# Eighteen gate and up tiles as pairs of seven products, and a down projection in six passes

## The chip, the core and the metric

The kernel runs on one core of a Trainium2 chip. The metric is the device time of one execution in microseconds; three runs of the kernel before gave 896.15, 896.58 and 896.68, a median of 896.58.

## What is computed

One layer of a decoder, for 520 token columns: 512 of a prompt and one each of 8 sample sequences. Three mixers (pooling, a gated recurrence, chunked gating) share an input projection and are merged; an output projection and a residual follow; then comes the channel mixer, and a last norm. The change is in the channel mixer, which computes, for x after the second norm (width 1024, inner width 3072):

```
g = conv3(x @ wg)              # depthwise over time, width 3, with bias
h = gelu_tanh(g) * (x @ wu)
out = residual + h @ wd        # then the final RMS norm, to the output y
```

All of it is fp32. The second norm divides each token by its root mean square; a gain per feature is folded into x. The state of the convolution is an output too.

## The kernel before

Features lie on the 128 partitions and tokens along the free axis. The 520 tokens are two halves of TH = 260 columns. An fp32 product is made of three products of rounded parts (type F32R): weight high by activation high, weight high by activation low, weight low by activation high. `mm` (lines 115 to 123) issues these for one k of 128 input features: three weight operands by two halves, six matmuls of 128x260 (line 122). A tile of 128 output features with 8 k takes 48 matmuls.

Weights come as chunks of up to 128x1024 fp32 (8 k of one output tile). `Chunk.load` (line 100) issues the DMA from SP into a `raw` buffer; `Chunk.high` (line 106) lets ACT copy it into `wh`; `Chunk.low` (line 112) lets DVE subtract, `wl = raw - wh`. `run_jobs` issues the jobs, one output tile each, in the order in which `job` was called; before a job's matmuls it issues the load, the high and the low of the chunks that lie LOADS = 3, HLEAD = 3 and LLEAD = 2 places ahead. So the queues of SP, ACT and DVE are filled in the order in which the program is written. Each engine runs its queue in order, and an instruction that waits holds all behind it. Work that isn't urgent is put off by `after(n, fn)` until the job counter has gone n further.

A job's sums lie in one PSUM tile of shape [128, 2, 512]: two banks, one per half of the tokens (`PS`, line 70). There are four such tiles. Activations lie in 61 buffers of 128x536.

The channel mixer: `fg_post` (651 to 658) takes the sums of a gate tile off (DVE, times the norm factor). `fg_rest` (660 to 671) makes the convolution: ACT scales and adds the bias (663), DVE adds the two shifted terms (665, two instructions) and the sample columns (667); ACT makes the gelu (669) and DVE multiplies by the norm factor (670). `u2_post` (687) multiplies the up tile's sums by it and splits the result into `h_h` (ACT, 261) and `h_l` (DVE, 262). `dn_post` (692) adds the sums of a down tile to the residual x1, which stays in SBUF. The jobs (726 to 739) go: gate tiles m and m + 1, up tiles m and m + 1, for m up to 11; then a pass of the down projection over these 12 k, 8 output tiles j; then the other 12 m and the second pass. Tiles 6 and 7 of that pass are made for the first half of the tokens, then for the second, so that the final norm of the first half (`sums(0)` and `last(0)`, lines 712 to 724) runs between.

```
        n = 8 if p == 0 else 6
        for js, halves in ((range(n), (0, 1)), (range(n, 8), (0,)), (range(n, 8), (1,))):
            for j in js:
                mid = (TAIL, lambda: n2.append(sums(0))) if halves == (1,) and j == 6 else None
                mid = (0, lambda: last(0, n2.pop())) if halves == (1,) and j == 7 else mid
```

Of the kernel before, what the change touches and what calls it, by code (L numbers as in the profile page):

```python
# [22 lines left out]
KD = D // P  # L23
DP = 512
# [3 lines left out]
HALF = MF // 2  # L28
KW = 6
# [17 lines left out]
# columns of the packed states: h0 (j b), conv (j r b), ffn (m r b), pool (g b r)  # L47
# [5 lines left out]
def trunk_kernel(ctx: ExitStack, tc: tile.TileContext, t: dict, o: dict):  # L53
    nc = tc.nc
    v, s, g, te = nc.vector, nc.scalar, nc.gpsimd, nc.tensor

# [3 lines left out]
    pp = ctx.enter_context(tc.tile_pool(name="pp", bufs=4, space=PSUM))  # L60
    ctx.enter_context(tc.manual_schedule())
# [16 lines left out]
    # ------------------------------------------------------------------ loads  # L78
# [69 lines left out]
    jobs, order = [], []  # L148

    def job(parts, post, pre=None, halves=(0, 1), mid=None):  # L150
        """An output tile: parts [(chunk, tile of the chunk, moving operands by k)], and
        post(psum) that takes the sums off; mid = (k, fn) runs fn before that k"""
        jobs.append((parts, post, pre, halves, mid))
        for c, _, _ in parts:
            if c not in order:
                order.append(c)

    def run_jobs():
        ahead = [(LOADS, "raw", Chunk.load), (HLEAD, "h", Chunk.high), (LLEAD, "l", Chunk.low)]
        at = [0] * 3  # L160
        for n0 in [0, *range(2, len(jobs))]:
            group = jobs[n0:n0 + (2 if n0 == 0 else 1)]
# [3 lines left out]
            i = max(order.index(c) for parts, *_ in group for c, _, _ in parts)  # L166
            for n, (lead, what, fn) in enumerate(ahead):
                while at[n] <= min(i + lead, len(order) - 1):
                    if not hasattr(order[at[n]], what):
                        fn(order[at[n]])  # L170
                    at[n] += 1
            pss = [PS("pj") for _ in group]
            ops = [[(c, a, X, k) for c, a, X in parts for k in range(c.nk)] for parts, *_ in group]
            for n, each in enumerate(zip(*ops)):
                for (c, a, X, k), ps, (_, _, _, halves, mid) in zip(each, pss, group):
                    if mid and mid[0] == n:
                        mid[1]()
                    mm(ps, c.w(k, a), X(k), n == 0, n == len(ops[0]) - 1, halves)
            for ps, each, (_, post, _, halves, _) in zip(pss, ops, group):
                now[0] += len(each) / 8 * len(halves) / 2  # L180
# [10 lines left out]
    # ------------------------------------------------------------------ constants  # L191
# [20 lines left out]
    # state parts of the sample tokens' convolutions  # L212
# [12 lines left out]
    def constants():  # L225
# [8 lines left out]
        # old rows of the sample states  # L234
# [4 lines left out]
    # 4 softplus(-lambda) = 4 (max(-lambda, 0) + log1p(exp(-|lambda|)))  # L239
# [18 lines left out]
    # ------------------------------------------------------------------ helpers  # L258
# [56 lines left out]
    def rstd_psum(r, name):  # L315
        """[m, n] to all partitions, along the tokens"""
# [12 lines left out]
    # ------------------------------------------------------------------ norm 1  # L329
# [15 lines left out]
    # ------------------------------------------------------------------ branch B: conv, RG-LRU  # L345
# [114 lines left out]
    # ------------------------------------------------------------------ branch A: pooling  # L460
# [56 lines left out]
    # ------------------------------------------------------------------ gates and merges  # L517
# [31 lines left out]
    # ------------------------------------------------------------------ branch C: chunked gating  # L549
# [59 lines left out]
    # ------------------------------------------------------------------ branch B: gate, merge  # L609
# [19 lines left out]
    for j in range(8):  # L629
        job([(Chunk(t["w_pb"][j], KD), 0, lambda k: yb[k])], lambda ps, j=j: pb_post(j, ps))  # L630
# [14 lines left out]
    # ------------------------------------------------------------------ channel mixer  # L645
# [5 lines left out]
    def fg_post(m, ps):  # L651
# [5 lines left out]
        v.tensor_mul(two(ext[:, 2:]), acc(ps), two(rs2[0]))  # L657
        fg_rest(m, ext)

    def fg_rest(m, ext):  # L660
# [9 lines left out]
        v.tensor_mul(y, y, rs2[0])  # L670
        fy[m] = y

    def g_post(m, ps):
# [17 lines left out]

    def dn_post(p, j, ps, halves):
        if len(halves) == 2:
            v.tensor_add(two(x1[j]), acc(ps), two(x1[j]))  # L694
            if p == 1:
                if j == 0:
                    nc.scalar.dma_start(o["small"], small)
                    s.activation(root, ones, AF.Sqrt)
                st3[0] = square_add(st3[0], x1[j], f"x2q{j}")
# [26 lines left out]
    for p in range(2):  # L726
        for i in range(HALF // 2):
            for m in (p * HALF + 2 * i, p * HALF + 2 * i + 1):
                job([(Chunk(t["wg"][m], KD), 0, lambda k: xg2[k])], lambda ps, m=m: g_post(m, ps))
            for m in (p * HALF + 2 * i, p * HALF + 2 * i + 1):  # L730
                job([(Chunk(t["wu"][m], KD), 0, lambda k: xg2[k])], lambda ps, m=m: u2_post(m, ps))
        cs = [[(Chunk(t["wd"][p, j, q], KW), 0, lambda k, o=p * HALF + q * KW: hh[o + k]) for q in range(2)]
              for j in range(8)]
        n = 8 if p == 0 else 6
        for js, halves in ((range(n), (0, 1)), (range(n, 8), (0,)), (range(n, 8), (1,))):
            for j in js:
                mid = (TAIL, lambda: n2.append(sums(0))) if halves == (1,) and j == 6 else None
                mid = (0, lambda: last(0, n2.pop())) if halves == (1,) and j == 7 else mid
                job(cs[j], lambda ps, p=p, j=j, halves=halves: dn_post(p, j, ps, halves), None, halves, mid)
# [30 lines left out]
NA, RAW, HS, LS, LOADS, HLEAD, LLEAD = 61, 4, 5, 4, 3, 3, 2  # L770
# [96 lines left out]
```

## Time and profile before

| What | us |
| --- | --- |
| median of three runs | 896.58 |
| the profiled execution's span, first to last instruction | 895.0 |
| PE busy | 884.0 (99%) |
| DVE busy | 525.2 (59%) |
| ACT busy | 344.0 (38%) |
| POOL busy | 56.1 (6%) |

The profile shows one execution, whose span is 895.0 us; its time with what lies around the span isn't given apart, so the median of the runs, 1.6 us more, stands for it. The shares are averages over the whole span. DMA moved 86.12 MB, and the mean granted TensorE clock was 0.996 of full speed. POOL sends three small DMAs of its own; SP sends all the weights.

### The profile page before, as it was taken

What the parts mean: (1) busy time and instruction counts of PE and PEld (TensorE: products, weight loads), DVE (VectorE), ACT (ScalarE), POOL (GpSimd) and SP (SyncE); (2) the same over time, 40 slices, a digit from 0 to 9 for tenths busy, and PEclk for the clock granted to TensorE, in tenths of its full rate; (3) what the DMA queues carried; (4) which work ended last, traced back from release to release, by engine and by line L of the source; (5) the groups of instructions that cost most, each with busy time, mean ns of one, the idle gap of its engine ahead of it and who ended that gap; (6) DMA issues with size and microseconds to landing.
All of it is one profiled execution on the core that took longest, in us unless ns stands there. A gap on an engine that the chain in (4) does not pass through costs nothing.

```text
span 895.0 us, 16824 instructions
## 1 busy us (share of the span) xinstructions
PE 884.0 (99%) x7358; PEld 880.8 (98%) x7358; DVE 525.2 (59%) x779; ACT 344.0 (38%) x456; POOL 56.1 (6%) x93
## 2 busy tenths in 40 slices
PE   9999999999999999999999999999999999999995
PEld 8999999999999999999999999999999999999995
DVE  5897998689665442155555666653234555554345
ACT  7554573776342342222334433332122333333210
POOL 1403311111100000000000000000000000000000
PEclk9999999999999999999999999999999999999998
DMA  9423233133232223222321422222332223323212
GB/s 293 152 99 107 73 106 98 57 96 95 72 118 72 94 92 122 71 72 95 95 94 48 131 89 90 88 71 90 106 113 77 95 94 94 95 71 116 74 37 96
DMA packets 28298, 86.12 MB, mean 96 GB/s; under 512 B 3112, under 2 KB 6312, under 8 KB 28200
## 3 DMA queue, kind: packets, MB, share of 16 engines
q1 hardware_dynamic: 26752, 83.21, 29.1%
q10 hardware_dynamic: 1376, 1.44, 0.5%
q8 instruction: 58, 0.95, 0.4%
q0 software_dynamic: 96, 0.39, 0.1%
q14 instruction: 16, 0.13, 0.0%
HBM read 82.63 MB, written 2.79 MB: 95 GB/s over the span
## 4 chain that ended last, share of the span: by engine, by line
PE 98%; DVE 1%; DMA 0%; ACT 0%; issue 0%; DVEq 0%
PE pj L122 95%; PE lru L122 1%; DVE y L722 1%; PE vm L581 0%; DMA par<-in_par 0%; PE po L122 0%; PE vt L574 0%; PE n30p L293 0%; DVE x2q L705 0%; DVE x L703 0%; PE n1p L293 0%; PE nvp L293 0%; PE n2p L293 0%; ACT xg_h L756 0%; PE n31p L293 0%; DVE n L309 0%
## 5 line engine op out<-in xcount | busy, mean ns | idle before, releaser
L112 DVE TENSOR_TENSOR wl<-raw,wh 128x1024 fp32r<-128x1024 f32 (+2 forms) x162 | 182.4, 1136 | 32.5 <-ACT wh L106 32.2
L106 ACT ACTIVATE wh<-raw 128x1024 fp32r<-128x1024 f32 (+2 forms) x162 | 156.7, 975 | 58.5 <-PE pj L122 55.5
L122 PE MATMUL pj<-x_h,wh 128*128 128x260 f32 x768 | 154.6, 283 | 0.0
L122 PE MATMUL pj<-x_h,wl 128*128 128x260 f32 x768 | 154.3, 282 | 0.0
L122 PE MATMUL pj<-x_l,wh 128*128 128x260 f32 x768 | 154.3, 282 | 0.0
L122 PE MATMUL pj<-xn_h,wh 128*128 128x260 f32 x704 | 142.1, 283 | 0.0
L122 PE MATMUL pj<-xn_l,wh 128*128 128x260 f32 x704 | 141.8, 283 | 0.0
L122 PE MATMUL pj<-xn_h,wl 128*128 128x260 f32 x704 | 141.5, 282 | 0.0
L122 PEld LDWEIGHTS pj<-x_h,wl 128*128 128x128 f32 x768 | 118.5, 188 | 0.0
L122 PEld LDWEIGHTS pj<-x_l,wh 128*128 128x128 f32 x768 | 118.1, 188 | 0.0
L122 PEld LDWEIGHTS pj<-x_h,wh 128*128 128x128 f32 x768 | 117.9, 188 | 0.0
L122 PEld LDWEIGHTS pj<-xn_h,wl 128*128 128x128 f32 x704 | 108.5, 188 | 0.0
L122 PEld LDWEIGHTS pj<-xn_h,wh 128*128 128x128 f32 x704 | 108.4, 189 | 0.0
L122 PEld LDWEIGHTS pj<-xn_l,wh 128*128 128x128 f32 x704 | 108.3, 188 | 0.0
L122 PE MATMUL pj<-h_h,wl 128*128 128x260 f32 x384 | 81.3, 283 | 0.0
L122 PE MATMUL pj<-h_h,wh 128*128 128x260 f32 x384 | 81.3, 283 | 0.0
L122 PE MATMUL pj<-h_l,wh 128*128 128x260 f32 x384 | 81.1, 282 | 0.0
L122 PEld LDWEIGHTS pj<-h_h,wl 128*128 128x128 f32 x384 | 60.9, 188 | 0.0
L122 PEld LDWEIGHTS pj<-h_l,wh 128*128 128x128 f32 x384 | 60.8, 188 | 0.0
L122 PEld LDWEIGHTS pj<-h_h,wh 128*128 128x128 f32 x384 | 60.8, 188 | 0.0
L694 DVE TENSOR_TENSOR x<-pj,x 128x520 f32<-128x520 f32 x14 | 9.8, 699 | 77.2 <-PE pj L122 77.2
L665 DVE SCALAR_TENSOR_TENSOR fc<-fg,par,fc 128x512 f32<-128x512 f32 x48 | 36.1, 752 | 18.9 <-ACT fc L663 18.0
(277 smaller groups left out, 1208.7 us busy)
## 6 DMA issues: line engine op xcount, KB each, us to landing
raw<-in_w_in SPq DMA_DIRECT2D x50, 512.0 KB, 3.6
raw<-in_wg SPq DMA_DIRECT2D x24, 512.0 KB, 3.5
raw<-in_wu SPq DMA_DIRECT2D x24, 512.0 KB, 3.5
raw<-in_wd SPq DMA_DIRECT2D x32, 384.0 KB, 3.1
raw<-in_w_pb SPq DMA_DIRECT2D x8, 512.0 KB, 3.5
raw<-in_w_o SPq DMA_DIRECT2D x8, 512.0 KB, 3.6
x<-in_x SPq DMA_DIRECT2D x8, 260.0 KB, 4.6
raw<-in_w_pa SPq DMA_DIRECT2D x4, 512.0 KB, 3.4
```

What stands on the lines that cost most here:

```text
L106: s.activation(self.h[:, q], self.raw[:, q], AF.Copy)
L112: v.tensor_sub(self.l[:, q], self.raw[:, q], f(self.h[:, q]))
L122: te.matmul(ps[:, h, :TH], ww, xx[:, h * TH:(h + 1) * TH], start=first and n == 0, stop=last and n == 2)
L665: v.scalar_tensor_tensor(y[:, :SEQ], ext[:, r:r + SEQ], pc("fcw", r * MF + m), y[:, :SEQ], op0=ALU.mult, op1=ALU.add)
L694: v.tensor_add(two(x1[j]), acc(ps), two(x1[j]))
L722: v.scalar_tensor_tensor(y[:, j - j0, :], x1[j][:, c], pc("gf", j), ps[:, 0, :TH], op0=ALU.mult, op1=ALU.mult)
```

## The change

Gate tiles 6 to 23 become nine pairs, and so do up tiles 6 to 23. The two tiles of a pair are a 2 by 2 block product: two output tiles by two halves of the tokens, and the 8 k as two halves of 4 k. Seven products of such blocks are made in place of eight (Winograd's form of Strassen's algorithm). The moving operands are sums and differences of normalised activations X0 to X8, made once in `operands()`; the weights are h1 (as loaded), h2 and h3 (sums that DVE makes) and h0 (a half, as loaded). A product is 12 matmuls of 128x260: 4 k by three part products.

- In `run_pair` the products P0, P2, P4 and P6 lie in bank 0 of a PSUM tile `pa`, P1 in bank 1 of the same tile, P3 and P5 in a tile `pc`. ACT copies four partial sums off (line 252): A1 after P0, A2 after P2, C1 after P3, A3 after P4. DVE makes c21 (bank 1 minus A1) after P1, then c12 (from SBUF) and c22; c11 is taken off after P6.
- The low part of h1 and h0, and of the weights of gate and up tiles 0 to 5, is made without DVE: a negated copy of the high part (POOL for h1 and h0, ACT for tiles 0 to 5), and then an accumulating DMA from POOL that adds the weights from DRAM.
- The down projection runs in six passes of 4 k. Pass p - 1 lies between the pairs of pass p: two down tiles behind each gate pair and two behind each up pair. For passes 0 to 4 ACT copies the sums off (line 946) and an accumulating DMA from POOL adds them to the residual, which now lies in DRAM. SP loads that back ahead of the last pass.
- In the last pass tiles 0 to 3 are made whole, then tiles 4 to 7 for the first half of the tokens, then for the second.
- Gate tiles 4 to 23 read normalised activations, so that the two multiplications by the norm factor fall away for them.
- There are 55 activation buffers in place of 61, and 5 of `wl` in place of 4.

```diff
+        PRODUCTS = ((("h1", 0), 0, 0), (("h1", 1), 1, 1), (("h3", 0), 2, 0), (("h2", 0), 3, 2),
+                    (("h2", 1), 4, 0), (("h3", 1), 5, 2), (("h0", 0), 6, 0))
...
+    def low_by_dma(eng, l, h, src):
+        if eng is s:
+            s.activation(l, f(h), AF.Copy, scale=-1.0)
+        else:
+            eng.tensor_scalar(l, f(h), -1.0, None, op0=ALU.mult)
+        nc.gpsimd.dma_start(l, src, accum_op=ALU.add)
...
+        def high1(self):
+            h, l = self.new("h1")
+            s.activation(h, self.raw[1], AF.Copy)
+            low_by_dma(NEG, l, h, self.src[1])
...
+        def steps(self):
+            return ((-3.5, self.load), (-2.2, self.high1), (-1.75, self.sums), (-1.3, lambda: self.high("h3")),
+                    (-1.05, lambda: self.high("h2")), (-0.8, self.high0), (-0.8, lambda: self.low("h3")),
+                    (-0.55, lambda: self.low("h2")))
...
+    def run_pair(n):
+        pair, X, out = pairs[n]
+        af, c = PS("pa"), PS("pc")
+        bank = (af[:, 0, :TH], af[:, 1, :TH], c[:, 0, :TH])
+        m, k = A("m"), A("k")
+        kept = {"A1": m[:, :TH], "A2": m[:, TH:], "A3": k[:, :TH], "C1": k[:, TH:]}
+        seen, t0 = [0, 0, 0], now[0]
+        for i, (b, ops) in enumerate(pair.products(X)):
+            for j, (w, x) in enumerate(ops):
+                for e, (ww, xx) in enumerate(((w[0], x[0]), (w[0], x[1]), (w[1], x[0]))):
+                    te.matmul(bank[b], ww, xx, start=seen[b] + j + e == 0, stop=i >= (6, 1, 5)[b] and j == 3 and e == 2,
+                              skip_group_check=True)
+            seen[b] += 1
+            now[0] = t0 + 0.25 * (i + 1)
+            if (b, seen[b]) in ((0, 1), (0, 2), (0, 3), (2, 1)):
+                s.activation(kept["AFC"[b] + str(seen[b])], bank[b], AF.Copy)
+            for a, fn in {1: ("c21", lambda: (bank[1], kept["A1"])), 4: ("c12", lambda: (kept["A3"], kept["C1"])),
+                          5: ("c22", lambda: (bank[2], kept["A2"])), 6: ("c11", lambda: (bank[0], None))}.items():
+                if a == i:
+                    out(fn[0], *fn[1]())
...
+            if n == "c11":
+                s.activation(o_, a, AF.Copy)
+                fg_rest(m, ext[0])
+                return
+            v.tensor_sub(o_, a, b)
+            if n == "c22":
+                after(0.2, lambda: fg_rest(m + 1, ext[1]))
...
     def dn_post(p, j, ps, halves):
+        if p < NP - 1:
+            y = A(f"dn{j}")
+            s.activation(two(y), acc(ps), AF.Copy)
+            nc.gpsimd.dma_start(x1d[:, j, :], y, accum_op=ALU.add)
+            return
...
+            if halves == (1,):
+                mid = {4: (3, lambda: n2.append(sums(0))), 6: (3, lambda: last(0, n2.pop()))}.get(j)
...
+    for p in range(NP):
+        for i in range(2):
+            m = p * KW + 2 * i
+            wg_jobs(m, m >= MN)
+            wd_jobs(p - 1, (4 * i, 4 * i + 1))
+            wu_jobs(m, m >= MN)
+            wd_jobs(p - 1, (4 * i + 2, 4 * i + 3))
+    wd_jobs(NP - 1, range(4))
+    for h in range(2):
+        for j in range(4, 8):
+            wd_job(NP - 1, j, (h,))
```

The order of the instructions on the engines, at three places. First PE at the start of a gate tile before (tile 10); `pj` is the tile's PSUM, `x1..h` and `x1..l` the parts of the moving operand, and "waits" names the engines or queues whose semaphores an instruction waits for.

```order
L122 MATMUL pj_6742<-x17_l_5439,wh_6552 128x260 x2
L122 MATMUL pj_6742<-x17_h_5438,wl_6620 128x260 x2
L122 MATMUL pj_6808<-x10_h_4998,wh_6618 128x260 [waits PE_49,Activation_49]
L122 MATMUL pj_6808<-x10_h_4998,wh_6618 128x260
L122 MATMUL pj_6808<-x10_l_4999,wh_6618 128x260 x2
L122 MATMUL pj_6808<-x10_h_4998,wl_6680 128x260 [waits DVE_49]
L122 MATMUL pj_6808<-x10_h_4998,wl_6680 128x260
L122 MATMUL pj_6808<-x11_h_5060,wh_6618 128x260 x2
```

And PE in the changed kernel at the gate pair of tiles 6 and 7, where its products P0, P1, P2 and P3 begin (X00 and X01 belong to P0, X1 to P1, X2 to P2, X3 to P3).

```order
L247 MATMUL pa_6525<-X00_h_6270,wh_6372 128x260 [waits DVE_49,Activation_49,Pool_49]
L247 MATMUL pa_6525<-X00_l_6271,wh_6372 128x260 [waits Pool_49]
...
L247 MATMUL pa_6525<-X01_h_6306,wl_6373 128x260
L247 MATMUL pa_6525<-X1_0h_5958,wh_6372 128x260 [waits Activation_49]
...
L247 MATMUL pa_6525<-X1_1h_5960,wl_6373 128x260
L247 MATMUL pa_6525<-X2_0h_6111,wh_6431 128x260 [waits DVE_49]
L247 MATMUL pa_6525<-X2_0l_6112,wh_6431 128x260
...
L247 MATMUL pa_6525<-X2_1h_6113,wl_6432 128x260
L247 MATMUL pc_6526<-X3_0h_6048,wh_6453 128x260 [waits PE_49]
L247 MATMUL pc_6526<-X3_0l_6049,wh_6453 128x260
```

Before, a tile waited at its start and at its first low part. Now the first matmul of P1 waits for ACT (its copy A1 of bank 0), and that of P2 for DVE (its c21 from bank 1), in each of the 18 pairs; P3's wait on PE is for the earlier user of `pc`.

Second, ACT's queue before, around gate tiles 8 and 9 (`fc` is the convolution and the gelu, `h` the product's high part).

```order
L663 ACTIVATE fc8_6543<-fg8_6539,par_77 128x512 [waits DVE_49,Pool_49]
L669 ACTIVATE fc8_6543<-fc8_6543 128x520 [waits DVE_49]
L106 ACTIVATE wh_6552<-raw_6550 128x1024 [waits DMAHW7_49,PE_49,Activation_49]
L663 ACTIVATE fc9_6609<-fg9_6605,par_77 128x512 [waits DVE_49,Pool_49]
L669 ACTIVATE fc9_6609<-fc9_6609 128x520 [waits DVE_49]
L106 ACTIVATE wh_6618<-raw_6616 128x1024 [waits DMAHW0_49,PE_49,Activation_49]
L261 ACTIVATE h8_h_6672<-fc8_6543 128x520 [waits DVE_49]
L106 ACTIVATE wh_6678<-raw_6676 128x1024 [waits DMAHW1_49,PE_49,Activation_49]
L261 ACTIVATE h9_h_6732<-fc9_6609 128x520 [waits DVE_49]
L106 ACTIVATE wh_6738<-raw_6736 128x1024 [waits DMAHW2_49,PE_49,Activation_49]
```

And in the changed kernel, from the gate pair of tiles 8 and 9 to the up pair behind it (`dn` are the down tiles' sums; `m` from `pa_7131` are A1 and A2 of the up pair).

```order
L907 ACTIVATE fg8_7011<-pa_6927 128x260 [waits PE_49,Activation_49]
L804 ACTIVATE fc8_7046<-fg8_7011,par_79 128x512 [waits DVE_49,Activation_49,Pool_49]
L810 ACTIVATE fc8_7046<-fc8_7046 128x520 [waits DVE_49]
L179 ACTIVATE wh_7052<-sum_6992 128x1024
L804 ACTIVATE fc9_7056<-fg9_6958,par_79 128x512
L810 ACTIVATE fc9_7056<-fc9_7056 128x520 [waits DVE_49]
L165 ACTIVATE whq_7075<-raw_6877 128x512 [waits DMAHW2_49]
L946 ACTIVATE dn0_7097<-pj_7062 128x520 [waits PE_49]
L116 ACTIVATE wh_7114<-raw_7030 128x1024 [waits DMAHW4_49]
L946 ACTIVATE dn1_7128<-pj_7101 128x520 [waits PE_49]
L252 ACTIVATE m_7133<-pa_7131 128x260 [waits PE_49]
L252 ACTIVATE m_7133<-pa_7131 128x260 [waits DVE_49,PE_49]
```

Before, the gelu of a tile stood between copies of weights. Now the two convolutions, the two gelus, three copies of weights and two of down sums stand between c11 of the gate pair and A1 of the up pair.

Third, DVE's queue in the tail before, behind the first half's sums (`n30` is the norm of the first half).

```order
L311 TENSOR_TENSOR n30l_9838<-n302_9836,n30h_9837 65x4 [waits DVE_49]
L300 TENSOR_TENSOR n30d1_9840<-ident_84,n30l_9838 65x260 [waits DVE_49]
L703 TENSOR_TENSOR x6_75<-pj_9812,x6_75 128x260 [waits PE_49]
L705 TENSOR_TENSOR x2q61_9875<-x6_75 128x260 [waits DVE_49]
L707 TENSOR_TENSOR x2q0_9276<-x2q0_9276,x2q61_9875 128x260 [waits DVE_49]
L722 SCALAR_TENSOR_TENSOR y00_9882<-x0_69,par_77,n30b_9879 128x260 [waits PE_49]
L722 SCALAR_TENSOR_TENSOR y01_9885<-x1_70,par_77,n30b_9879 128x260
```

And in the changed kernel at the same place.

```order
L441 TENSOR_TENSOR n30l_10354<-n302_10352,n30h_10353 65x4 [waits DVE_49]
L430 TENSOR_TENSOR n30d1_10356<-ident_86,n30l_10354 65x260 [waits DVE_49]
L958 TENSOR_TENSOR xe4_10133<-pj_10331,xe4_10133 128x260 [waits PE_49]
L960 TENSOR_TENSOR x2q41_10370<-xe4_10133 128x260 [waits DVE_49]
L962 TENSOR_TENSOR x2q0_10169<-x2q0_10169,x2q41_10370 128x260 [waits DVE_49]
L958 TENSOR_TENSOR xe5_10135<-pj_10373,xe5_10135 128x260 [waits PE_49]
L960 TENSOR_TENSOR x2q51_10387<-xe5_10135 128x260 [waits DVE_49]
L962 TENSOR_TENSOR x2q0_10169<-x2q0_10169,x2q51_10387 128x260 [waits DVE_49]
L977 SCALAR_TENSOR_TENSOR y00_10403<-xe0_10125,par_79,n30b_10400 128x260 [waits PE_49]
L977 SCALAR_TENSOR_TENSOR y01_10406<-xe1_10127,par_79,n30b_10400 128x260
```

Before, one tile's residual stood between the norm and the first half's y; now it is two tiles', and two more follow behind the eight y.

## Rows read from the trace of the kernel before

**Rows 1.** The profile page: busy us (share) and instructions; then the chain by engine

```profile
PE 884.0 (99%) x7358; PEld 880.8 (98%) x7358; DVE 525.2 (59%) x779; ACT 344.0 (38%) x456; POOL 56.1 (6%) x93
...
PE 98%; DVE 1%; DMA 0%; ACT 0%; issue 0%; DVEq 0%
```

**Rows 2.** The chain that ended last, in order of time: start us, us, engine, what

```profile
36.87 34.63 PE pj L122 x288
...
480.17 395.37 PE pj L122 x3300
875.54 0.89 PE n30p L293 x16
...
884.91 0.65 PE n31p L293 x8
```

**Rows 3.** Timeline of PE at its last dense matmuls: start us, us, engine, line, instruction, out<-in

```profile
883.53 0.28 PE L122 MATMUL pj<-h_l,wh 128*128 128x260 f32 x1
883.65 0.28 PE L122 MATMUL pj<-h_h,wl 128*128 128x260 f32 x1
```

**Rows 4.** Groups of instructions by line and shape: busy us, mean ns, then idle before them

```profile
L112 DVE TENSOR_TENSOR wl<-raw,wh 128x1024 fp32r<-128x1024 f32 x122 | 150.0, 1232 | 31.9 <-ACT wh L106 31.6 <-issue 0.3
...
L106 ACT ACTIVATE wh<-raw 128x1024 fp32r<-128x1024 f32 x122 | 127.6, 1049 | 22.7 <-PE pj L122 21.0 <-DMA raw<-in_w_in 1.7
...
L663 ACT ACTIVATE fc<-fg,par 128x512 f32<-128x512 f32 x24 | 19.6, 817 | 70.5 <-DVE fg L657 66.0 <-DVE fg L681 2.3 <-DVE small L661 2.1
...
L261 ACT ACTIVATE h_h<-fc 128x520 fp32r<-128x520 f32 x24 | 15.3, 639 | 65.9 <-DVE fc L689 65.9
...
L522 ACT ACTIVATE gt<-pj 128x520 f32<-128x520 f32 x24 | 14.5, 605 | 82.2 <-PE pj L122 78.0 <-issue 4.2
```

**Rows 5.** Timeline of ACT in the channel mixer, 520 to 527 us

```profile
521.23 0.82 ACT L663 ACTIVATE fc<-fg,par 128x512 f32<-128x512 f32 x1 [4.22 <-DVE fg L657]
523.79 0.64 ACT L669 ACTIVATE fc<-fc 128x520 f32<-128x520 f32 x1 [1.74 <-DVE fc L667]
524.33 1.05 ACT L106 ACTIVATE wh<-raw 128x1024 fp32r<-128x1024 f32 x1
```

**Rows 6.** Timeline of DVE in the tail, from 878 us

```profile
878.21 0.42 DVE L300 TENSOR_TENSOR n30d<-ident,n30l 65x260 fp32r<-65x260 f32 x1
879.44 0.43 DVE L703 TENSOR_TENSOR x<-pj,x 128x260 f32<-128x260 f32 x1 [0.80 <-PE pj L122]
...
880.71 3.25 DVE L722 SCALAR_TENSOR_TENSOR y<-x,par,n30b 128x260 f32<-128x260 f32 x8
883.97 0.43 DVE L703 TENSOR_TENSOR x<-pj,x 128x260 f32<-128x260 f32 x1
884.43 0.43 DVE L705 TENSOR_TENSOR x2q<-x 128x260 f32<-128x260 f32 x1
```

**Rows 7.** DMA issues: out<-in, queue, operation, KB each, us from issue to landing

```profile
raw<-in_wg SPq DMA_DIRECT2D x24, 512.0 KB, 3.5
...
out_pool_old<-in_state_pool POOLq DMA_DIRECT2D x1, 224.0 KB, 5.3
```

**Rows 8.** Groups of POOL's instructions by line and shape, as rows 4

```profile
L396 POOL TENSOR_SCALAR q<-q 128x520 f32<-128x520 f32 x8 | 8.8, 1096 | 108.6 <-DVE q L395 108.6
...
L235 POOL DMA_DIRECT2D out_pool_old<-in_state_pool x1 | 0.8, 776 | 0.0
```

**Rows 9.** Busy time in one-us windows near the end: PE, PEld, DVE, ACT, POOL, granted clock

```profile
883.00:884.00 1.00, 1.00 (x13) 1.00 (x12) 1.00 (x4) 0.00 (x0) 0.00 (x0) 1.00 0.93 312
...
887.00:888.00 1.00, 0.51 (x2) 0.31 (x2) 0.75 (x3) 0.00 (x0) 0.00 (x0) 1.00 0.03 7
888.00:889.00 1.00, 0.35 (x1) 0.06 (x1) 0.61 (x2) 0.00 (x0) 0.00 (x0) 0.51 0.00 0
```

**Rows 10.** Timelines of DVE and then of POOL, 95 to 112 us

```profile
105.07 1.90 DVE L112 TENSOR_TENSOR wl<-raw,wh 128x1024 fp32r<-128x1024 f32 x1
...
104.82 4.43 POOL L482 TENSOR_TENSOR ps<-ps 128x524 f32<-128x524 f32 x3
```

More of the change, by code (lines that the diff above doesn't have):

```diff
@@ L23 @@
 KD = D // P
+KW = 4
 DP = 512
@@ L27 @@
 MF = FF // P
-HALF = MF // 2
-KW = 6
 EPS = 1e-6
@@ L148, in trunk_kernel, with at, pair_job @@
     jobs, order = [], []
+    pairs = {}
+    def at(t, fn):
+        later.append((t, len(later) + done[0], fn))
+    def pair_job(pair, X, out):
+        pairs[len(jobs)] = (pair, X, out)
+        jobs.append(None)
+    def run_pair(n):
[18 more added lines that the diff above has]
+                    out(fn[0], *fn[1]())
+            run_later(now[0] + 1e-6)
     def job(parts, post, pre=None, halves=(0, 1), mid=None):
@@ L154, in job @@
         for c, _, _ in parts:
-            if c not in order:
+            if c not in order and not c.timed:
                 order.append(c)
@@ L159, in run_jobs @@
         ahead = [(LOADS, "raw", Chunk.load), (HLEAD, "h", Chunk.high), (LLEAD, "l", Chunk.low)]
-        at = [0] * 3
+        begun = [0] * 3
+        t1 = 0
+        for n, e in enumerate(jobs):
+            if e is None:
+                for dt, fn in pairs[n][0].steps():
+                    at(t1 + dt, fn)
+                t1 += 1.75
+                continue
+            parts, _, _, halves, _ = e
+            for c, _, _ in parts:
+                if c.timed and not hasattr(c, "raw") and not hasattr(c, "due"):
+                    c.due = t1
+                    for lead, fn in zip((4, 3, 2.9) if c.by_dma else (3, 2, 1.5), (c.load, c.high, c.low)):
+                        at(t1 - lead, fn)
+            t1 += sum(c.nk for c, _, _ in parts) / 8 * len(halves) / 2
         for n0 in [0, *range(2, len(jobs))]:
+            if n0 in pairs:
+                run_pair(n0)
+                continue
             group = jobs[n0:n0 + (2 if n0 == 0 else 1)]
@@ L165, in run_jobs @@
                     pre()
-            i = max(order.index(c) for parts, *_ in group for c, _, _ in parts)
+            timed = group[0][0][0][0].timed
+            i = max([order.index(c) for parts, *_ in group for c, _, _ in parts if not timed], default=-9)
             for n, (lead, what, fn) in enumerate(ahead):
[L168 to L171, printed above, removed]
+                while begun[n] <= min(i + lead, len(order) - 1):
+                    if not hasattr(order[begun[n]], what):
+                        fn(order[begun[n]])
+                    begun[n] += 1
             pss = [PS("pj") for _ in group]
@@ L178, in run_jobs @@
                     mm(ps, c.w(k, a), X(k), n == 0, n == len(ops[0]) - 1, halves)
+                if timed and n < len(ops[0]) - 1:
+                    now[0] += len(halves) / 16
+                    run_later(now[0] + 1e-6)
             for ps, each, (_, post, _, halves, _) in zip(pss, ops, group):
-                now[0] += len(each) / 8 * len(halves) / 2
+                now[0] += (1 if timed else len(each)) / 8 * len(halves) / 2
                 post(ps)
@@ L656, in fg_post @@
             return ext
-        v.tensor_mul(two(ext[:, 2:]), acc(ps), two(rs2[0]))
+        if m < MN:
+            v.tensor_mul(two(ext[:, 2:]), acc(ps), two(rs2[0]))
+        else:
+            s.activation(two(ext[:, 2:]), acc(ps), AF.Copy)
         fg_rest(m, ext)
@@ L682, in g_post @@
                 fg_rest(i, x)
+            after(0.25, operands)
     n2 = [None]
@@ L724, in last @@
             (nc.sync if i % 2 == 0 else nc.scalar).dma_start(o["y"][:, j0:j0 + n, c], y)
[L726 to L735, printed above, removed]
-            for j in js:
-                mid = (TAIL, lambda: n2.append(sums(0))) if halves == (1,) and j == 6 else None
-                mid = (0, lambda: last(0, n2.pop())) if halves == (1,) and j == 7 else mid
-                job(cs[j], lambda ps, p=p, j=j, halves=halves: dn_post(p, j, ps, halves), None, halves, mid)
+    XP = [op_of(n) for n in range(7)]
```

189 lines of the change are left out of this document (174 added, 15 removed).

## The prediction

> **What bounds it now.** I read the page first, for the engine that is full, then the chain of waits, for whether its time is work, then timelines, for the price of one step. PE is busy 884.0 us and is 98% of the chain that ended last [rows 1]. Within the chain 288 matmuls take 34.63 us and 3300 take 395.37 us [rows 2], so a matmul costs 0.120 us, with no pause for another engine. Two things follow: each matmul left out saves 0.120 us, and each wait put into PE's queue is paid in full, since nothing else is behind it. A single matmul takes 0.28 us from start to end while the next starts after 0.12 us [rows 3]. So a PE that must wait for the result of its last matmul loses 0.28 - 0.12 = 0.16 us of draining ahead of any handoff.
>
> **What is saved.** A pair before is 96 matmuls (2 tiles of 48) and now 84 (7 products of 12). That is 12 x 18 = 216 fewer, 216 x 0.120 = 25.9 us. The down projection has as many matmuls in six passes as in two.
>
> **What is added, first part: two waits in each pair.** The order of PE's queue shows that P1's first matmul waits for ACT's copy A1, and P2's for DVE's c21, since both banks are one tile. P0 ends just ahead of P1, so this isn't hidden. P1's wait is draining 0.16, handoff to the reader 0.04 (a matmul ends at 883.65 + 0.28 = 883.93 [rows 3] and DVE starts at 883.97 [rows 6]), the copy, and the handoff back, 0.05 (884.86 to 884.91 [rows 2, 6]). The copy of 128x260 from PSUM isn't in the trace. The copy of 128x520 is 0.605; two SBUF copies, 1.049 for 1024 columns and 0.639 for 520, give 0.81 ns per column [rows 4], so 0.605 - 0.21 = 0.39. Its ends are 0.30 (half of 0.605) and 0.605 (no gain). P1 loses 0.16 + 0.04 + 0.39 + 0.05 = 0.64 us. P2's wait has a DVE subtraction of 128x260 in place of the copy, 0.43 [rows 6]: 0.68 us. P3's wait is for an earlier user of the other PSUM tile, long done. P4, P5 and P6 wait for copies issued a whole product (1.44 us) earlier, so there are some 0.4 us to spare. A pair with two such waits takes 84 x 0.12 + 0.64 + 0.68 = 11.40 us.
>
> **Second part: ACT's queue ahead of each up pair.** I count from the start of a gate pair. It ends at 11.40; the two down tiles behind it take 48 x 0.12 = 5.76, so the up pair starts at 17.16, and P1 could start one product later, at 18.60. A1 of that up pair stands on ACT behind everything in the order's rows:
> - c11 starts at 11.60 and ends at 11.99; the first convolution starts at 12.01.
> - A convolution's start to its gelu's start is 523.79 - 521.23 = 2.56 us, as DVE's two shifted terms lie between; the gelu to the next start is 0.54 us [rows 5], which is 0.10 less than its own 0.64.
> - I take off this 0.10 for each ACT instruction that follows another: copies of 1024 columns 0.95, of 512 (1.049 - 512 x 0.81 ns = 0.63) 0.53, of down sums 0.51.
> - So: gelu 14.57, h2's copy 15.11, second convolution 16.06, its gelu 18.62, h0's copy 19.16, down sums 19.69, down weights 20.20, down sums 21.15, A1 from 21.66 to 22.05, P1 at 22.10.
>
> P1 waits 22.10 - 18.60 = 3.50 us instead of 0.64. Behind the up pair stand two high parts in place of convolution and gelu, and no step there waits 2.56 us, so ACT has caught up by the next gate pair. A cycle of a gate and an up pair then loses 0.64 + 0.68 + 3.50 + 0.68 = 5.50 us, and nine cycles 49.5 us.
>
> **Third part: the tail.** Before, 60 matmuls followed the sums for the first half's norm; now 39 do, so 21 x 0.12 = 2.5 us of PE's work stand ahead of that point. From its start to the end the kernel took 895.0 - 875.54 = 19.46 us [rows 2]. Now: the norm's steps on DVE end 3.09 us later (878.63); two tiles' residual steps, 1.27 each (879.44 to 880.71); eight y, 3.26 (to 883.97); tile 6, 1.27; tile 7 up to the second sums, 0.94 (to 884.91); from there to the end 10.09, as before [rows 2, 6]. That makes 3.09 + 2.54 + 3.26 + 1.27 + 0.94 + 10.09 = 21.19 us. The tail costs 21.19 - 19.46 + 2.5 = 4.2 us; if DVE's order didn't matter it would cost nothing.
>
> **What costs nothing.** Copies and additions of the down sums (ACT, POOL's DMAs): nobody waits for the DMA before the last pass, and the copies' place on ACT is counted above. DVE's four sums per pair and low parts: before, DVE was busy 59% [rows 1], and it lost the two multiplications of each gate tile; without that cover it would delay c21, at 1.23 us for each low part [rows 4]. POOL's negations can slow DVE: beside POOL's additions a low part took 1.90 us [rows 10] and not 1.23; they fall mostly where ACT's queue is late anyhow.
>
> **The sum.** 895.0 - 25.9 + 49.5 + 4.2 = 922.8 us of span; the median of the runs lies 1.6 us above the span, so 924.4 us. My own range for this case: 915 (copies of 0.30, ACT gaining another 0.5 us per cycle, no cost in the tail) to 935 (copies of 0.605, no overlap of 0.10 on ACT).
>
> **Rivals.**
> *Accumulating DMAs that land late.* The trace has none. h1's low part is needed by the third matmul of the next pair. In a gate pair h1's copy follows A2 and ends near 7.2 us; POOL's negation of 1024 columns takes two of 1.10 (520 columns), the DMA's issue 0.78 [rows 8], so the issue ends at 10.2, and 7.2 us are left to 17.4; the up pair leaves about as much. A plain load of 512 KB lands in 3.5 us, POOL's own DMA of 224 KB in 5.3 [rows 7], and by size that would be 12.1 for 512 KB. I take about 6, nearer to the first, since POOL's 224 KB came from DRAM to DRAM, so no loss. At 12.1 each gate pair waits 4.9 us and each up pair 4.9 less some 2.9 that its ACT backlog hides: 9 x (4.9 + 2.0) = 62, giving 986 us.
> The Trainium skill, page DMA: Bandwidth & Descriptors, section on the anatomy of one DMA on the SWDGE path, fits 2.0 us plus bytes over 436 GB/s for one DMA. By that 512 KB would be an estimated 3.2 us and this rival would fall; but the 224 KB row has 5.3 where the fit has 2.5, so the trace does not agree.
>
> *The clock falls in the gaps.* In the tail the granted clock was 1.00 up to 888 us and 0.51 in the next microsecond, the lower level, 1.2 GHz, about 4 us after the last dense matmul at 883.93 [rows 3, 9], with only a few small ones between. The gap of 3.50 us is about that long. If it fell and P1 and P2 ran at the lower level, 24 matmuls would cost 0.12 more each, 2.9 us x 9 = 26: 950 us. Against: 3.5 is under 4, and PE is dense on both sides.
> The Trainium skill, TensorE: Matmul & The Clock Gate, section on HAM oscillation, describes a kernel with idle stretches of a few microseconds between bursts, each of which started at the lower clock. By that rule this rival is the forecast; here only the end of the kernel shows such a fall.
>
> *No backlog.* If ACT reached A1 in time, only the bare waits stayed: 18 x 1.32 = 23.8, and 895.0 - 25.9 + 23.8 + 4.2 + 1.6 = 898.7, 2.1 us over the median and at the edge of what can be told from no change. It needs ACT's queue between c11 and A1 to be 2.9 us shorter, with two steps of 2.56 us that DVE sets.
>
> *Faster.* P1 and P2 write where nobody reads just then, and if their waits are met while matmuls still drain, the saving stays. It decides below (25.9 - 4.2) / 18 = 1.21 us lost per pair. With the bare copy and subtraction alone, 0.82 per pair, the time is 895.0 - 25.9 + 14.8 + 4.2 + 1.6 = 889.7; with no loss 874.9. For it speaks ACT's 38% [rows 1]; against it, that the waits stand in the order's rows and draining is a measured 0.16.
>
> That the saving isn't made at all can't be: the queue holds 216 matmuls less.
>
> **How the numbers follow.** Forecast 0.62, clock 0.11, late DMAs 0.12, no backlog 0.05, faster 0.10. The predicted time is the forecast's, 924.4. The range, 897 to 952, takes in the forecast's 915 to 935, no backlog and the clock; left out are the faster case (0.10) and most of the late DMAs (0.10). A measurement of this kernel can tell 0.2%, 1.8 us: faster 0.10, same 0.05, slower 0.85.
>
> **What would show it.** In the profile after: PE's idle ahead of P1 and P2 named as released by ACT and DVE, 0.64 and 0.68 us, and about 3.5 us ahead of each up pair's P1; PE busy about 858 us; ACT without a pause from c11 to the up pair's A1. Wrong would be PE waiting at a pair's third matmul for a DMA queue, a granted clock under 1.00 after the gaps, or idle of PE below 1.2 us per pair.

## The result, and the profile after

The changed kernel takes 961.36 us (median of 4 runs, 958.49 to 965.64) against 896.63 us for the kernel before: a ratio of 1.0725, with a 95% interval from 1.0697 to 1.0754. It is slower, as forecast, but by 64.7 us and not by 28; the time lies outside the range. The profiled execution's span is 963.9 us.

The page of the changed kernel, its busy times, its granted clock in 40 slices and its chain, answers to [rows 1].

```profile
PE 893.8 (93%) x7142; PEld 880.6 (91%) x7142; DVE 576.4 (60%) x894; ACT 438.5 (45%) x633; POOL 235.5 (24%) x237
...
PEclk9999999999999999999999988987999879999797
...
PE 75%; DVE 9%; ACT 9%; issue 4%; DMA 2%; POOL 0%; DVEq 0%; ACTq 0%
```

PE executes fewer matmuls and yet reads busier than 884.0 us; the clock row says why: of its last 17 slices, eight show a 7 or an 8, that is, a mean clock under 0.9. PE's share of the chain fell from 98% to 75%: now other engines release it. The waits of PE, largest first (us in total, times, longest):

```profile
PE pa L247 <- ACT m L252: 35.0, 18, 3.4
PE pa L247 <- DVE c L929: 5.3, 9, 0.6
PE pa L247 <- DVE fg L910: 5.2, 9, 0.6
PE pa L247 <- DMA wl<-in_wg: 5.1, 1, 5.1
...
PE pj L200 <- DVE wl L125: 3.9, 1, 3.9
```

The first three are the forecast's: 18 waits for A1, 9 and 9 for c21. The waits of 5.1 and 3.9 us are single ones, at the third matmul of the first pair and in the first down tiles. Cycles of a gate and an up pair on PE's timeline (start us, us; in brackets the idle ahead and its releaser):

```profile
604.47 0.39 PE L247 MATMUL pa<-X_0h,wh 128*128 128x260 f32 x1 [0.54 <-ACT m L252]
...
606.76 0.39 PE L247 MATMUL pa<-X_0h,wh 128*128 128x260 f32 x1 [0.58 <-DVE fg L910]
...
624.78 0.39 PE L247 MATMUL pa<-X_0h,wh 128*128 128x260 f32 x1 [3.42 <-ACT m L252]
...
627.14 0.59 PE L247 MATMUL pa<-X_0h,wh 128*128 128x260 f32 x1 [0.59 <-DVE c L929]
...
644.89 0.39 PE L247 MATMUL pa<-X_0h,wh 128*128 128x260 f32 x1 [0.47 <-ACT m L252]
...
665.15 0.58 PE L247 MATMUL pa<-X_0h,wh 128*128 128x260 f32 x1 [3.37 <-ACT m L252]
...
686.28 0.39 PE L247 MATMUL pa<-X_0h,wh 128*128 128x260 f32 x1 [0.54 <-ACT m L252]
...
706.59 0.39 PE L247 MATMUL pa<-X_0h,wh 128*128 128x260 f32 x1 [3.43 <-ACT m L252]
...
708.91 0.39 PE L247 MATMUL pa<-X_0h,wh 128*128 128x260 f32 x1 [0.59 <-DVE c L929]
...
723.99 0.39 PE L247 MATMUL pa<-X_0h,wh 128*128 128x260 f32 x1 [0.48 <-ACT m L252]
```

P1 and P2 of the gate pair at 604.47 and 606.76 wait 0.54 and 0.58 us, P1 and P2 of the up pair at 624.78 and 627.14 wait 3.42 and 0.59. The idle is counted from the modelled end of the last matmul; with the draining of 0.16 us of [rows 3] these are 0.70, 0.74, 3.58 and 0.75 us. From one gate pair's P1 to the next it takes 40.42 us (604.47 to 644.89), 41.39 (to 686.28) and 37.71 (to 723.99). The 264 matmuls of a cycle, at 0.12 us each, are worth 31.68 us. The 37.7 are a cycle at full clock, and they hold 6.0 us of waits.

What the longer cycles have beyond that shows in one-us windows of the first (the length of the window; busy time of PE, PEld, DVE, ACT and POOL; then the granted clock):

```profile
620.00:621.00 1.00, 1.00 (x11) 1.00 (x10) 0.96 (x2) 0.00 (x0) 0.00 (x0) 1.00 0.00 0
622.00:623.00 1.00, 0.00 (x0) 0.00 (x0) 1.00 (x2) 1.00 (x4) 0.38 (x1) 1.00 0.00 0
...
626.00:627.00 1.00, 0.54 (x5) 0.27 (x3) 0.35 (x2) 0.00 (x0) 1.00 (x3) 0.64 0.90 156
627.00:628.00 1.00, 0.86 (x4) 0.87 (x5) 0.96 (x3) 0.00 (x0) 0.96 (x2) 0.50 0.92 221
632.00:633.00 1.00, 1.00 (x7) 1.00 (x6) 0.00 (x0) 0.26 (x1) 1.00 (x1) 0.50 1.03 199
...
634.00:635.00 1.00, 1.00 (x11) 1.00 (x10) 0.15 (x1) 0.57 (x2) 0.70 (x2) 1.00 0.37 148
```

PE idled from 621.36 to 624.78. The clock was still granted in full in that time and a microsecond beyond, then fell to 0.50, the lower level of 1.2 GHz, until about 633. There the matmuls of P2 and P3 run at half speed: P2's first takes 0.59 us in the rows at 627.14 and 0.39 at 708.91, where the clock stayed up. Over the nine cycles the clock fell in seven, at 2.7 to 3.7 us each; the cycles from 686 and from 806 us had the same idle of 3.4 us and kept it.

### The profile page after: what moved, and what is told of

Read it like the earlier page. It is cut to its first block, busy times and chain, and to the rows that moved or that the text cites. A ratio compares the mean times of both kernels' runs of the same rounds, so it can differ in the third digit from the quotient of the medians.

```text
span 963.9 us, 16992 instructions
## 1 busy us (share of the span) xinstructions
PE 893.8 (93%) x7142; PEld 880.6 (91%) x7142; DVE 576.4 (60%) x894; ACT 438.5 (45%) x633; POOL 235.5 (24%) x237
## 4 chain that ended last, share of the span: by engine, by line
PE 75%; DVE 9%; ACT 9%; issue 4%; DMA 2%; POOL 0%; DVEq 0%; ACTq 0%
PE pj L200 53%; PE pa L247 13%; PE pc L247 6%; DVE fc L806 3%; ACT fc L804 2%; ACT wh L116 2%; DVE wl L125 1%; PE lru L200 1%; ACT fc L810 1%; ACT dn L946 1%; DMA wl<-in_wg 1%; ACT wh L179 1%; DVE y L977 1%; ACT whq L165 1%; DMA x<-in_x 1%
## 5 line engine op out<-in xcount | busy, mean ns | idle before, releaser
L125 DVE TENSOR_TENSOR wl<-raw,wh 128x1024 fp32r<-128x1024 f32 (+1 forms) x106 | 124.2, 1177 | 38.6 <-ACT wh L116 38.6
L116 ACT ACTIVATE wh<-raw 128x1024 fp32r<-128x1024 f32 (+1 forms) x118 | 117.7, 1004 | 10.5 <-PE pj L200 7.7
L247 PE MATMUL pa<-X_0h,wh 128*128 128x260 f32 x108 | 38.5, 357 | 45.5 <-ACT m L252 35.0
L247 PEld LDWEIGHTS pa<-X_0h,wh 128*128 128x128 f32 x108 | 23.8, 220 | 53.7 <-ACT m L252 38.8
L97 POOL TENSOR_SCALAR wl<-wh 128x1024 fp32r<-128x1024 f32 x18 | 50.3, 2792 | 75.3 <-ACT wh L160 75.3
L97 POOL TENSOR_SCALAR wlq<-whq 128x512 fp32r<-128x512 f32 x18 | 34.6, 1923 | 120.0 <-ACT whq L165 120.0
L252 ACT ACTIVATE m<-pa 128x260 f32<-128x260 f32 x36 | 13.9, 387 | 100.2 <-PE pa L247 100.2
L652 ACT ACTIVATE gt<-pj 128x520 f32<-128x520 f32 x24 | 14.5, 605 | 83.0 <-PE pj L200 83.0
L183 DVE TENSOR_TENSOR wl<-sum,wh 128x1024 fp32r<-128x1024 f32 x36 | 46.3, 1325 | 0.0
```

The costliest lines, as they stand in the source:

```text
L97: eng.tensor_scalar(l, f(h), -1.0, None, op0=ALU.mult)
L116: s.activation(self.h[:, q], self.raw[:, q], AF.Copy)
L183: v.tensor_sub(l, self.s[n], f(h))
L247: te.matmul(bank[b], ww, xx, start=seen[b] + j + e == 0, stop=i >= (6, 1, 5)[b] and j == 3 and e == 2, skip_group_check=True)
L252: s.activation(kept["AFC"[b] + str(seen[b])], bank[b], AF.Copy)
L652: s.activation(two(y), acc(ps), AF.Sigmoid)
```

## The experiments

Theory: what the forecast lacks is the low clock, and the long idle ahead of an up pair's P1 causes it; ACT is late there because it waits for DVE between convolution and gelu. Rivals: the clock falls from the short pauses or the load of DMA and POOL; ACT is short of time; the six passes and accumulating DMAs cost the time.

**A tile of its own for P1's bank.**

```diff
-        af, c = PS("pa"), PS("pc")
-        bank = (af[:, 0, :TH], af[:, 1, :TH], c[:, 0, :TH])
+        af, ag, c = PS("pa"), PS("pb"), PS("pc")
+        bank = (af[:, 0, :TH], ag[:, 0, :TH], c[:, 0, :TH])
```

> The bank of P1 becomes a PSUM tile of its own, so P1 no longer waits for the copy A1; P2 does, because it adds to bank 0. Theory (the late A1 idles PE and the long idle lowers the clock): the two short waits of a gate pair go, the wait of an up pair moves to P2 and shrinks from 3.4 to about 2.0 us, and an idle of 2 us leaves the clock at 1.00: 9 x 3 = 27 us less idle and about 34 us less at the low clock, near 900 us. Rival (the clock falls for another reason, the short waits apart: the load of DMA and POOL, or the single-bank products): the idle goes, the low clock stays, near 934 us.

914.24 us, ratio 1.0193 (1.0173 to 1.0213). PE's waits for ACT in the pairs:

```profile
PE pa L247 <- ACT m L252: 17.6, 9, 2.0
```

Nine in place of 18, none over 2.0 us, and behind only one of these nine (at 755 us) did the clock fall, for 3 us. The time fell by 47.1 us, where the rival had 27. It is 14 us above the 900 expected, mostly since the low clock had been priced at 34 us, too much, as the run after next shows; four waits of up to 0.9 us for the low part of h0 are new.

**The second convolution behind A1.**

```diff
-                after(0.2, lambda: fg_rest(m + 1, ext[1]))
+                after(1.5, lambda: fg_rest(m + 1, ext[1]))
```

> Only the convolution and gelu of the second tile of a gate pair are put behind A1 of the up pair on ACT. Theory: A1 comes on time, the wait of 3.4 us becomes 0.5 as in a gate pair, and the clock stays at 1.00: 9 x 2.9 = 26 us of idle and some 34 us of low clock go, near 901 us. Rival (the clock falls with the pauses of 0.5 us or the load): 26 us go and the clock still falls, near 935 us. Rival two (ACT is simply short of time): the convolution behind A1 now delays A2 and the 3 us come back at P4, near 961 us.

922.64 us, ratio 1.0287 (1.0266 to 1.0307). PE's waits in the pairs:

```profile
PE pa L247 <- DVE c L929: 9.4, 9, 1.1
PE pa L247 <- ACT m L252: 8.8, 18, 0.5
```

A1 is on time, as expected (0.5 at the longest). But c21 of the up pairs now waits up to 1.1 us and not 0.6, as DVE's terms of the moved convolution stand ahead of it. The clock stayed at 1.00 in the cycles. The time is 39 us lower, but 22 above the 901 expected: the same overpriced clock (34 against the 17.7 of the next run) and 4 us of the later c21 are most of it. Rival two, a shortage of ACT, would have left 961.

**Unused matmuls in the gap.**

```diff
+            if fill and i == 1:
+                for _ in range(fill):
+                    te.matmul(c[:, 1, :TH], ops[0][0][0], ops[0][1][0], start=True, stop=True)
...
-            pair_job(Pair(t["wu"][m], t["wu"][m + 1]), XP, wu_out(m))
+            pair_job(Pair(t["wu"][m], t["wu"][m + 1]), XP, wu_out(m), 24)
```

> Behind P0 of each up pair stand 24 matmuls into an unused bank, 2.9 us that PE would idle; their result is used by nobody. Theory: A1 comes when it came, PE waits for it only some 0.5 us, the clock stays at 1.00 in every up pair, and the run takes the 34 us less that the low clock cost, near 927 us with 216 matmuls more. Rival (the low clock comes from something else in the pair): 961 us or more, granted clock as before.

943.7 us, ratio 1.0521 (1.0500 to 1.0542). PE's queue holds 216 matmuls more and the kernel is 17.7 us faster. Windows of the changed kernel, four us each:

```profile
622.00:626.00 4.00, 1.22 (x10) 1.22 (x11) 2.83 (x3) 2.73 (x6) 3.08 (x3) 1.00 0.41 131
626.00:630.00 4.00, 3.41 (x18) 3.14 (x17) 2.92 (x5) 0.00 (x0) 1.96 (x3) 0.53 0.96 202
630.00:634.00 4.00, 4.00 (x24) 4.00 (x24) 0.00 (x0) 1.72 (x3) 2.43 (x1) 0.61 1.03 225
```

And of this one, at the same place:

```profile
622.00:626.00 4.00, 2.88 (x22) 2.67 (x22) 2.60 (x4) 0.49 (x2) 3.42 (x4) 1.00 0.74 206
626.00:630.00 4.00, 4.00 (x36) 4.00 (x35) 1.45 (x4) 2.29 (x5) 2.00 (x1) 1.00 1.08 195
630.00:634.00 4.00, 4.00 (x35) 4.00 (x35) 2.06 (x5) 1.94 (x3) 1.69 (x2) 1.00 0.85 208
```

With the gap filled the clock stays at 1.00 in the cycles, and from the second on each takes 37.7 us. So P1 starts as late as before, ACT is as late, and all that changed is the clock: it is caused by the idle, which is thereby shown. The size was missed, 17.7 and not 34: the 34 had been read from windows by adding up what the clock lacked, also where PE idled. In the changed kernel's profile the seven falls cost 21.8 us, from an up pair's P1 to what stands behind it, against the cycles that kept the clock (the last of them against this run); the profiled execution is the slowest of the four (965.64 us), the others had mean clocks of 0.961 to 0.968 and not 0.958.

**Six of them.** The same with 6 in place of 24.

> The changed kernel with 6 unused matmuls in place of 24 behind P0 of each up pair: PE's idle there becomes about 2.7 us. If an idle of 2.7 us leaves the clock as one of 2.0 does, the cycles take 37.7 us each with no low clock and the run is near 944 us, as with 24; if it lowers the clock as one of 3.4 us does, the run is near 960 us.

951.59 us (two runs, 949.75 and 953.43), ratio 1.0611 (1.0588 to 1.0635). It lies between the two times expected. Two up pairs of this run, P1 and P2 of each:

```profile
663.44 0.39 PE L250 MATMUL pa<-X_0h,wh 128*128 128x260 f32 x1 [2.65 <-ACT m L255]
...
665.75 0.39 PE L250 MATMUL pa<-X_0h,wh 128*128 128x260 f32 x1 [0.59 <-DVE c L932]
...
777.10 0.39 PE L250 MATMUL pa<-X_0h,wh 128*128 128x260 f32 x1 [2.70 <-ACT m L255]
...
779.77 0.58 PE L250 MATMUL pa<-X_0h,wh 128*128 128x260 f32 x1 [0.59 <-DVE c L932]
```

The same idle of 2.65 to 2.70 us ahead of P1 left the clock at 1.00 at 663 us (P2's first matmul 0.39) and lowered it at 777 us (0.58). That makes 3 falls behind the 9 waits, against 7 of 9 with 3.4 us, one of 9 with 2.0 (the run with the tile for P1's bank) and none with 0.5 (the run with 24). What tells cycles with the same idle apart was not found. Nor is the length of the idle alone shown to set the count: at 2.7 and 3.4 us a second idle of 0.6 us follows ahead of P2, at 2.0 us none does.

**Both edits.** The tile for P1's bank and the convolution behind A1.

> Both edits: P1's bank as a tile of its own, and the second tile's convolution behind A1. Theory: A1 is copied while P1 runs, so no pair waits; 45 us of idle and 34 us of low clock go, near 882 us, the two single waits of 3.9 and 5.1 us ahead of the first pair remain. Rival (clock falls under the load): 916 us. Rival two (the next wait takes their place, for DMAs of the low parts that now have less time): 890 to 900 us with PE waiting at the third matmul of a pair.

894.24 us, ratio 0.9966 (0.9953 to 0.9979): 0.3% faster than before. No wait for ACT or DVE is left in the pairs. Rival two was right on what comes next:

```profile
PE pa L247 <- DMA wl<-in_wg: 8.9, 7, 4.2
```

One of these seven is the first pair's 4.2 us; in six later gate pairs the low part of h1 lands 0.3 to 1.1 us late.

**Convolutions first, gelus after.** With P1's bank apart, `fg_rest` puts the gelu off (`after(0.1)` for the first tile of a pair, `after(0.2)` for the second), so ACT starts both convolutions before the first gelu; nothing stands behind A1.

```diff
+        fy[m] = y
+        def gelu():
             s.activation(y, y, AF.Gelu_apprx_tanh)
...
+            after(0.1 if m % 2 == 0 else 0.2, gelu)
```

> P1's bank a tile of its own, as in the run before; instead of putting the second tile's convolution behind A1, ACT starts both convolutions first and makes the gelus while DVE has done its two terms, so ACT no longer waits 2.56 us twice. Theory (ACT was late because it waited for DVE between convolution and gelu, not because it is short of time): A1 of the up pair comes on time, A2 and h1's copy too, so the waits of 0.3 to 1.1 us of gate pairs for h1's low part also go: about 889 us. Rival (the accumulating DMA itself is too slow for the place it has): these waits stay, 894 us.

888.82 us, ratio 0.9911 (0.9896 to 0.9926), as expected. Of the pairs' waits only the first pair's for a DMA is left, and PE is busy without a pause from 600 to 860 us at a clock of 1.00:

```profile
PE pa L247 <- DMA wl<-in_wg: 5.1, 1, 5.1
```

```profile
600.00:860.00 260.00, 260.00 (x2174) 260.00 (x2173) 170.72 (x263) 147.03 (x234) 122.76 (x107) 1.00 0.83 182
```

So ACT was not short of time; two waits of 1.74 us for DVE made it late.

**Single tiles again.** Pairs from tile 24 on, which means none.

```diff
-MN, MP = 4, 6
+MN, MP = 4, 24
```

> Gate and up tiles 6 to 23 as single tiles again; six passes, accumulating DMAs, the tail and normalised operands as in the change. Theory: 216 matmuls more and no waits inside a cycle, so 896.6 + 4.2 of the tail + 4 to 9 at the switch = 905 to 910 us, and the clock stays at 1.00 in the cycles. Rival (six passes and the DMAs of the low parts themselves cost the time, not the pairs): 930 us or more with a falling clock.

912.63 us, ratio 1.0176 (1.0156 to 1.0197), a little above the 905 to 910, with no wait in the cycles. The six passes, the tail and the switch cost 15.7 us together. Against the run above, which has the products and no waits between them after the first pair, the products save 23.8 us of the forecast's 25.9; the two runs' waits at the switch differ by about a microsecond.

**h1 earlier.**

```diff
-            return ((-3.5, self.load), (-2.2, self.high1), ...
+            return ((-3.5, self.load), (-2.7, self.high1), ...
```

> The same, and h1's copy on ACT with what follows (POOL's negation, the accumulating DMA) starts right behind A1 of the pair ahead, about 2.5 us earlier. Theory: all the waits for wl in pairs go, and the single wait of 4.2 us at the first pair shrinks to 1 or 2 us, so 885 to 887 us. Rival (POOL's queue, not the start of h1, sets the time): no change from the run above.

888.91 us, ratio 0.9912 (0.9897 to 0.9927): no change. The waits in question had gone already. The first pair's went from 5.1 us to 4.3 only, and DVE's low part for the first down tiles came 0.3 us later. The expectation was wrong about the first pair.

**The switch.** In addition X0's negation on ACT, and the first down weights a step earlier.

> The same, and at the switch to pairs: the negation of X0 on ACT in place of POOL, and the weights of the first down tiles one step earlier. Theory: the waits of 4.2 and 3.4 us ahead of the first pair fall under 1 us, and the low clock that follows them does not come: 878 to 882 us. Rival (DVE and ACT are short there, since the X operands are made then): another wait of the same length takes their place, 885 us or more.

886.28 us, ratio 0.9883 (0.9866 to 0.9899). It missed the 878 to 882 expected. The wait for DVE's low part is gone, but a wait of 2.1 us for an up tile's low part has come, and the first pair's is 3.6 us: the rival was right.

**The first pair's low part by DVE.** In addition DVE's subtraction for up tiles 4 and 5 and the first gate pair's h1.

> The run called switch, with the low parts of up tiles 4 and 5 and of the first gate pair's h1 made by DVE's subtraction in place of the negated copy and the accumulating DMA. Theory (near the switch the accumulating DMA's landing of about 7 us is the last link): the waits of 2.2 and 3.6 us go, and the low clock after them: 879 to 881 us. Rival (DVE is short there): other waits of 2 us or more, 884 us or more.

884.58 us, ratio 0.9863 (0.9847 to 0.9880). The waits of 2.1 and 3.6 us for DMAs went; others of 3.0 and 1.5 us came, released by ACT and DVE, as the rival had it. The first row is the tail's, as it was:

```profile
PE n31p L426 <- DVE x2q L972: 4.3, 1, 4.3
PE pa L250 <- ACT m L255: 3.0, 1, 3.0
...
PE pb L250 <- DVE fc L904: 1.5, 1, 1.5
```

**The tail.** In addition ACT squares the half tiles.

```diff
-        v.tensor_mul(q[:, c], x1[j][:, c], x1[j][:, c])
+        while held_q:
+            hc, hq = held_q.pop()
+            v.tensor_add(st3[0][:, hc], st3[0][:, hc], hq[:, hc])
+        s.activation(q[:, c], x1[j][:, c], AF.Square)
```

> The same, and in the tail ACT squares the half tiles, each square being added when the next tile comes, so that DVE has 0.43 us less per half tile. Theory (DVE's order sets the tail): PE's wait ahead of the second half's norm shrinks from 4.3 to about 2.7 us and the run is 1.6 us shorter than the one above. Rival (the residual's DMA or PE sets the tail): no difference.

882.64 us (881.05 to 884.05), ratio 0.9842 (0.9827 to 0.9857). PE's wait ahead of the second half's norm went from the 4.3 us above to:

```profile
PE n31p L426 <- DVE x2q L974: 3.1, 1, 3.1
```

The median fell by 1.9 us where 1.6 were expected; the two runs' ranges overlap by 0.5 us. The wait accounts for 1.2 us; the rest isn't shown to be the tail's, since behind the first pair's waits the clock fell in the profile of the run above and stayed at 1.00 in this one. This kernel makes the same products as the changed one and beats it and the kernel before.

## Why the prediction was wrong

**The saving** of 25.9 us was right, near enough: 23.8 us between the two runs with and without products.

**The waits of P1 and P2** were right in place and size. Forecast 0.64, 0.68, 3.50 and 0.68 us per cycle; measured 0.70, 0.74, 3.58 and 0.75. ACT's timeline from c11 of a gate pair to A1 of the up pair behind it:

```profile
614.30 0.39 ACT L907 ACTIVATE fg<-pa 128x260 f32<-128x260 f32 x1 [1.60 <-PE pa L247]
614.78 0.82 ACT L804 ACTIVATE fc<-fg,par 128x512 f32<-128x512 f32 x1
617.34 0.64 ACT L810 ACTIVATE fc<-fc 128x520 f32<-128x520 f32 x1 [1.74 <-DVE fc L808]
...
618.83 0.80 ACT L804 ACTIVATE fc<-fg,par 128x512 f32<-128x512 f32 x1
621.37 0.64 ACT L810 ACTIVATE fc<-fc 128x520 f32<-128x520 f32 x1 [1.74 <-DVE fc L808]
...
623.86 0.59 ACT L946 ACTIVATE dn<-pj 128x520 f32<-128x520 f32 x1
624.35 0.39 ACT L252 ACTIVATE m<-pa 128x260 f32<-128x260 f32 x1
```

From c11 to A1 it took 624.35 - 614.30 = 10.05 us; the forecast had 21.66 - 11.60 = 10.06, with each convolution 2.56 us ahead of its gelu. So ACT was late by the path that the forecast had worked out. Its sign "ACT without a pause" doesn't fit that working, which had these two waits for DVE inside its 2.56 us. The nine cycles lost 54 us to waits and not 49.5; the first matmul behind a wait shows 0.39 us and not 0.28 in the rows, four times a cycle, which is most of the difference.

**The step that failed is the choice between the forecast and the rival called "The clock falls in the gaps".** It had a chance of 0.11 because "3.5 is under 4, and PE is dense on both sides". The 4 us came from one fall in the tail [rows 3, 9], where a few small matmuls had run in between, so the comparison set no lower limit for an idle that lowers the clock. The forecast thus put the clock at nothing; in the run it cost 21.8 us in seven of the nine cycles, about 3.2 us behind the two single waits and about 1 us in the tail, 26.0 us in all. That the rival's price was 26 us is in part luck: it counted nine cycles at 2.9 us, and not seven at 3.1, nor the other places. The sign that the prediction had named for it, a granted clock under 1.00 after the gaps, was there. The Trainium skill, TensorE: Matmul & The Clock Gate, section on HAM oscillation, describes idle stretches between bursts after each of which the next burst starts slow. The trace agrees in part: in three cycles of nine the next matmuls started slow (0.58 us at 665.15), in four they slowed 1.0 to 1.5 us after the start, in two they did not. The prediction weighed that rule against one row that could not decide.

**A term was missing: the switch to pairs.** "What costs nothing" looked at the steady cycles only. Ahead of the first pair the X operands are made, and the chain of waits shows what was late (start us, us, what):

```profile
529.51 1.13 DVE wl L125
...
547.71 0.90 POOL x1d L947
548.60 2.85 POOL wl L97
...
551.75 8.55 DMA wl<-in_wg
```

DVE's low part for the first down tiles ended late, 3.9 us of waiting; and for the first pair POOL's issue of another DMA, its negation and a landing of 8.55 us came one behind another, 5.1 us of waiting. With 0.4 us at an earlier low part that makes about 9.3 us. The prediction had named PE waiting at a pair's third matmul for a DMA queue as a sign of being wrong; it came in this one pair of 18.

**The accumulating DMAs** were judged rightly for the cycles. KB and us to landing, of the changed kernel:

```profile
wl<-in_wg POOLq DMA_DIRECT2D x15, 512.0 KB, 6.0
wl<-in_wu POOLq DMA_DIRECT2D x15, 512.0 KB, 5.6
```

They land in 5.6 to 6.0 us, where about 6 was taken. In the cycles as they are none comes late; in the run with both edits, whose cycles are shorter, six did. POOL's negation of 1024 columns was dearer than the 2.20 us of the forecast:

```profile
L97 POOL TENSOR_SCALAR wl<-wh 128x1024 fp32r<-128x1024 f32 x18 | 50.3, 2792 | 75.3 <-ACT wh L160 75.3
```

The Trainium skill's fit (DMA: Bandwidth & Descriptors, the anatomy of one DMA on the SWDGE path) gave an estimated 3.2 us for a transfer of that size; the rows have 5.6 and 6.0, so for an accumulating one the trace does not agree.

**The tail**: from the first half's sums (941.67) to the end it took 22.23 us, the forecast had 21.19. Its eight y stood where the forecast put them:

```profile
947.30 3.25 DVE L977 SCALAR_TENSOR_TENSOR y<-xe,par,n30b 128x260 f32<-128x260 f32 x8
```

The 1.0 us beyond is the low clock again, at PE's last few matmuls.

**The sum again**: 895.0 - 25.9 + 54.2 (cycles) + 9.3 (switch) + 4.2 (tail) + 26.0 (clock) = 962.8, against a span of 963.9 us. Of the miss of 41.1 us, 26.0 are the clock, 9.3 the switch and 4.7 the size of the waits; 1.1 us are not accounted for.

## What to carry to other kernels

Where PE is full, read for every new wait what stands ahead of its releaser on that engine's queue: here a copy of 0.39 us came 3 us late behind two gelus that waited for DVE, and starting both convolutions first, with a tile of its own for P1's bank, took the delay away. An idle of PE costs its own length and may cost as much again in clock; a filler of unused matmuls tells the two apart in one run. A place where one pattern of work gives way to another needs a sum of its own.

## What the runs showed that was not expected

The clock's fall is not a fixed price. With dense matmuls on both sides, it came behind none of nine waits of 0.5 us in up pairs, behind one of nine at 2.0 us, three at 2.7 and seven at 3.4. In four of the seven it came after PE had resumed (at 626 us, the idle having ended at 624.78), and the matmuls were slow for some 7 us; in three it came while PE still idled, and they were slow for about 9. Filling idle time with 216 unused matmuls made a kernel 17.7 us faster.
